# A decoder step on one Trainium2 core: the sample group's attention as plain fp32 products in four column tiles

## The chip, the cores and the metric

The kernel runs on one core of a Trainium2 chip. A core has TensorE (PE in the profile, with its weight loads shown apart as PEld), VectorE (DVE), ScalarE (ACT), GpSimd (POOL), and queues that issue DMAs, most of them from SyncE (SP). The metric is device time in microseconds for one execution, as the median of several runs; lower is better.

## The reference, cut to what matters

The program is one layer of a decoder for a prompt group (1024 rows) and a sample group (8 rows, one new token each, with 4096 past tokens in a paged cache). All is fp32. The change touches the attention of the sample group, which is this part of the reference:

```python
def mla_sample(q_nope, q_rope, c_new, kr_new, pool_ckv, pool_krope, page_table, w_uk, w_uv):
    q_lat = jnp.einsum('bthd,lhd->bthl', q_nope, w_uk)
    past_c = pool_ckv[page_table].reshape(Bd, -1, KV_LORA)      # 8 x 4096 x 256
    past_r = pool_krope[page_table].reshape(Bd, -1, ROPE_DIM)   # 8 x 4096 x 32
    s_past = jnp.einsum('bthl,bkl->bhtk', q_lat, past_c) + jnp.einsum('bthr,bkr->bhtk', q_rope, past_r)
    s_new = jnp.einsum('bthl,bkl->bhtk', q_lat, c_new) + jnp.einsum('bthr,bkr->bhtk', q_rope, kr_new)
    ...
    s = jnp.concatenate([s_past.astype(jnp.float32) * MLA_SCALE, s_new], axis=-1)
    p = jax.nn.softmax(s, axis=-1).astype(c_new.dtype)
    o_lat = jnp.einsum('bhtk,bkl->bthl', p[..., :P], past_c) + jnp.einsum('bhtk,bkl->bthl', p[..., P:], c_new)
    return jnp.einsum('bthl,lhd->bthd', o_lat, w_uv).reshape(Bd, T, H * MLA_HEAD_DIM)
```

There are 8 heads. Keys and values of the prompt's memory, `mem_prompt @ w_xk` and `mem_prompt @ w_xv` (256 rows, 4 heads of 256 columns each), are computed in the same stage, and the layer norm of the convolution's output for its last tiles.

## The kernel before

The program runs its stages one after another: projections and convolution, the prompt group's attention, the sample group's attention (block `c2`, from L617), then the output projection, cross attention and feed-forward. A scheduler sets the order of the instructions on each engine from their dependencies and from the order in which the code gives them; buffers are tiles of pools with a fixed number of copies (`bufs`), and a tile waits until the last user of its copy is done. Most products are in a fast fp32 form, fp32r, of operands split in a rounded high part and the rest as low part (`split`, L136; the cast is `cast`, L127, the subtraction `lows`, L133).

Stage `c2`, for each batch row b of 8 and each of 8 groups g of 4 token tiles (128 tokens each):

- `gather_part` (L634) gathers a quarter of b's latents, 128 partitions x 2048 elements, with an indirect DMA that GpSimd issues; each parity of b has four buffers. `gather_rope` (L629) does the same for the rope keys.
- `score_group` (L711) transposes latents on PE, two banks of four 128x128 tiles (`trc`, L723), splits them into `ch` (ACT) and `cl` (DVE), and multiplies each into `main` with 128 stationary columns: the absorbed queries `qst`, hi and lo, sit in a window of zeros, so that the groups add up on disjoint rows of one PSUM bank (L728, L729). Rope keys go the same way after every fourth group (`trr`, `rh`, `rl`, into `rsc`, L740 and L741).
- `softmax` (L745) copies `main` and `rsc` out (`mr`), turns them with eight plain fp32 products against `summ` (`st`, L753 and L755), takes maximum, exponential and sum, and splits the weights in `pp`.
- `value_group` (L784) splits four token tiles of the latents, not transposed, into `cc` (casts on POOL, low parts on DVE and POOL) and multiplies them with `pp` as 16 stationary columns and 512 moving ones, hi and lo side by side (`pv`, L795). After every second group it gathers a part for b + 2. At the end `ob` is turned with `summ` (L805).

Values of b run beside scores of b + 1. `memory_kv` (L828) has eight heads (keys and values of four) of 48 fp32r products of 256 columns (L140 to L142), with weights cast on ACT and split on DVE; `conv_norm` (L421) norms the last four tiles of the convolution.

Of the kernel before, what the change touches and what calls it, by code (L numbers as in the profile page):

```python
# [9 lines left out]
F32 = mybir.dt.float32  # L10
# [49 lines left out]
def host_constants():  # L60
# [16 lines left out]
    summ = np.zeros((P, 64), np.float32)  # L77
    for a in range(P):
        summ[a, (a // 16) * 8 + a % 8] = 1.0
# [17 lines left out]
def decoder_step(ctx: ExitStack, tc: tile.TileContext, I: dict, O: dict):  # L97
# [11 lines left out]
    class Banks:  # L109
        """PSUM banks of a phase by tag; those that were taken longest ago go to the first tags"""  # L110
# [47 lines left out]

    # constants
# [12 lines left out]
    # residents of the mixer  # L172
# [19 lines left out]
    # memory keys and values; input projections; convolution  # L192
    with ExitStack() as c1:
# [4 lines left out]
        # the attention's half of mix holds small operands until its results come  # L198
# [3 lines left out]
        def to_T(src, rows, dh, dl, c0, he="a", le="v"):  # L202
            """src [rows, 1024] natural -> hi/lo columns c0.. of dh, dl [P, KD, *]"""
# [19 lines left out]
        def load_w(cols, apart=False):  # L223
            """columns of w_in as hi and lo; apart: each range of columns is split on its own"""
# [31 lines left out]
        def small_loads():  # L256
# [4 lines left out]
            # rows of the paged cache, as the gathers take them  # L261
# [13 lines left out]
            # convolution weights, transposed; the state's part of the sample group's convolution  # L275
# [126 lines left out]
        # depthwise convolution  # L402
# [18 lines left out]
    def conv_norm(i, pool_, ps, tag, bufs):  # L421
        """normalisation of the convolution's output over its channels, in place"""
# [7 lines left out]
        V.tensor_scalar(n[:rows], n[:rows], mv[:rows, 0:1], r[:rows], op0=ALU.subtract, op1=ALU.mult)  # L430
        t2 = ps.tile([P, NCT, P], F32, tag="tr", name="tl2")
# [12 lines left out]
    # attention of the prompt group  # L444
    with ExitStack() as c3:
# [145 lines left out]
        for n in range(len(seq) + LAG):  # L591
# [16 lines left out]
            if n in CLN:  # L608
                with tc.high_priority(offset=0):
                    conv_norm(CLN.index(n), ap_, ps, "sc", 1)  # L610
# [4 lines left out]
    # attention of the sample group over the paged cache  # L615
    with ExitStack() as c2:
        ps = Banks(tr=3, st=1, main=1, rsc=1, pv=1, mk=1)  # L617
# [15 lines left out]
        def gather_part(b, c):  # L633
            raw = (dp if b % 2 else ra).tile([P, 8, LAT], F32, tag="raw", bufs=4, name="craw")  # L634
# [8 lines left out]
        # absorbed queries  # L643
# [7 lines left out]
        main, rsc, probs, pvt = {}, {}, {}, {}  # L651

        def score_banks(b):
            main[b] = ps.tile([P, 512], F32, tag="main", name="main")
            rsc[b] = ps.tile([P, 4, P], F32, tag="rsc", name="rsc")

        score_banks(0)
# [8 lines left out]
        ukT = dp.tile([HD, H, LAT], F32, tag="cc", bufs=4, name="ukT")  # L666
# [15 lines left out]
        summ = dp.tile([P, 64], F32, name="summ")  # L682
        nc.sync.dma_start(summ, I["k_summ"])
        # scores of the new token, on every partition
# [14 lines left out]
        # hi | lo columns of the absorbed queries inside windows of zeros  # L699
        ZW, ZR = 112, 64  # L700
        qst = [de.tile([P, 2, 2 * ZW + 16], F32R, name=f"qst{j}") for j in range(2)]
        qrs = [de.tile([P, 2 * ZR + 64], F32R, name=f"qrs{j}") for j in range(2)]
        for j in range(2):
            G.memset(ff(qst[j]), 0.0)
            G.memset(ff(qrs[j]), 0.0)
        olT = kp.tile([P, 2, H, DB], F32, tag="qs", name="olT")

        def score_group(b, g):
            qw, qv = qst[b % 2], qrs[b % 2]
            if g == 0:  # L710
                gather_rope(b)  # L711
                V.tensor_copy(qw[:, :, ZW:ZW + 8], ql[:, :, b, :])
                V.tensor_tensor(qw[:, :, ZW + 8:ZW + 16], ql[:, :, b, :], ff(qw[:, :, ZW:ZW + 8]), op=ALU.subtract)
                for j in range(4):
                    r0, z0 = slice(j * RD, (j + 1) * RD), ZR + 16 * j
                    V.tensor_copy(qv[r0, z0:z0 + 8], qr[:, b, :])
                    V.tensor_tensor(qv[r0, z0 + 8:z0 + 16], qr[:, b, :], ff(qv[0:RD, ZR:ZR + 8]), op=ALU.subtract)
                if b:
                    score_banks(b)
            for k in range(2):  # L720
                t = ps.tile([P, 4, P], F32, tag="tr", name="trc")
                for j in range(4):
                    T.transpose(t[:, j, :], raws[b][g // 2][:, (g % 2) * 4 + j, k * P:(k + 1) * P], ident)  # L723
                ch = de.tile([P, 512], F32R, tag="ch", bufs=3, name="ch")
                cl = de.tile([P, 512], F32R, tag="cl", bufs=3, name="cl")
                split(ch, cl, t.rearrange("p a b -> p (a b)"), "a", "v")
                w = qw[:, k, ZW - 16 * g:ZW - 16 * g + P]
                T.matmul(main[b], w, ch, start=(g == 0 and k == 0), stop=False)  # L728
# [652 lines left out]
```

## Time and profile before

| what | value |
|---|---|
| median of 3 runs | 1978.37 us (1973.42 to 1978.55) |
| span of the profiled execution | 1981.0 us |
| PE busy in it | 1849.9 us, 93% |
| mean granted TensorE clock | 0.960 |
| stage `c2`, first PE instruction to the first of the next stage | 482.33 to 831.47 us |

The page of the profile gives the profiled execution's span, from the first to the last instruction, and no other time of it; the runs' times are of other executions. "Busy" is the time in which at least one instruction of an engine runs. Matmuls overlap their neighbours in the pipeline, so the mean duration of one is longer than the distance from its start to the start of the next. A plain fp32 product has two records. "Releaser" is the instruction whose end let a waiting one go.

### The profile page before, as it was taken

The numbers are of one execution on the slowest core, as the hardware profiler recorded it, in microseconds if no ns is written. First come the engines' busy times: TensorE is split into PE (matmuls) and PEld (weight loads), VectorE is DVE, ScalarE is ACT, GpSimd is POOL, SyncE is SP. The second block draws the span as 40 slices with busy tenths as digits, with TensorE's granted clock in tenths as the row PEclk, the third lists the DMA queues.
The fourth block names the chain that finished last, engine by engine and source line by source line (L and its number), as shares of the span: only waits on it lengthen the run. The fifth ranks groups of instructions, "written<-read, shape, count | busy, mean of one in ns | idle before, by whom it ended". The sixth has DMA issues, their size and how long they took to land.

```text
span 1981.0 us, 29364 instructions
## 1 busy us (share of the span) xinstructions
PE 1849.9 (93%) x11556; PEld 1687.1 (85%) x11556; DVE 1318.0 (67%) x2278; ACT 602.3 (30%) x1317; POOL 640.0 (32%) x636
## 2 busy tenths in 40 slices
PE   8857779998999989799999999999999999999997
PEld 8857777787877777587997787999999999999997
DVE  4999768888788777766547865755455555545447
ACT  3433457776533443411114400211111111111114
POOL 0779973225155545531104522200000101010002
PEclk9978989999998998799999999999999999999999
DMA  6002000005344531322433720211111111111102
GB/s 202 25 23 59 22 12 1 1 12 214 118 145 158 193 133 54 127 76 102 145 98 111 241 81 24 77 52 43 44 43 43 43 54 54 54 44 54 44 1 87
DMA packets 103205, 154.00 MB, mean 78 GB/s; under 512 B 8718, under 2 KB 79798, under 8 KB 98963
## 3 DMA queue, kind: packets, MB, share of 16 engines
q1 hardware_dynamic: 97307, 114.38, 18.4%
q0 software_dynamic: 5760, 37.75, 5.3%
q8 instruction: 91, 1.49, 0.3%
q14 instruction: 47, 0.39, 0.1%
HBM read 140.29 MB, written 12.29 MB: 77 GB/s over the span
## 4 chain that ended last, share of the span: by engine, by line
PE 72%; POOL 12%; DVE 7%; issue 5%; DMA 2%; ACT 2%; SPq 0%; DVEq 0%; POOLq 0%; ACTq 0%
POOL mix L411 7%; PE pd L141 6%; PE pd L142 6%; PE pd L140 6%; PE pu L140 6%; PE pu L141 6%; PE pu L142 6%; PE po L141 3%; PE po L142 3%; PE po L140 3%; PE trc L723 2%; DVE cc L134 2%; PE px L141 2%; PE px L140 2%; PE px L142 2%
## 5 line engine op out<-in xcount | busy, mean ns | idle before, releaser
L1294 DVE TENSOR_TENSOR YT<-YT,pd 128x344 f32<-128x344 f32 (+2 forms) x344 | 171.8, 504 | 232.1 <-PE pd L142 232.1
L141 PE MATMUL pd<-hl,dh 128*128 128x344 f32 (+2 forms) x800 | 251.4, 314 | 2.8 <-DVE hl L134 2.8
L142 PE MATMUL pd<-hh,dl 128*128 128x344 f32 (+2 forms) x800 | 251.4, 314 | 0.0
L140 PE MATMUL pd<-hh,dh 128*128 128x344 f32 (+2 forms) x800 | 250.3, 314 | 0.0
L140 PE MATMUL pu<-XHb,uh 128*128 128x344 f32 x768 | 246.4, 321 | 0.0
L141 PE MATMUL pu<-XLb,uh 128*128 128x344 f32 x768 | 246.0, 320 | 0.0
L142 PE MATMUL pu<-XHb,ul 128*128 128x344 f32 x768 | 245.9, 320 | 0.0
L1281 ACT ACTIVATE r<-pu 128x344 f32<-128x344 f32 x96 | 43.9, 459 | 425.3 <-PE pu L142 383.5
L131 POOL TENSOR_SCALAR dh<-draw 128x1024 fp32r<-128x1024 f32 x32 | 39.2, 1243 | 386.2 <-PE pd L141 385.3
L411 POOL TENSOR_TENSOR mix<-mix,tap 128x512 f32<-128x512 f32 (+1 forms) x120 | 160.4, 1337 | 8.2 <-ACT tap L410 0.8
L416 DVE SCALAR_TENSOR_TENSOR mix<-u,convw,mix 128x768 f32<-128x768 f32 (+1 forms) x120 | 153.9, 1328 | 0.3
L141 PEld LDWEIGHTS pd<-hl,dh 128*128 128x128 f32 x800 | 150.7, 188 | 3.1 <-DVE hl L134 3.1
L142 PEld LDWEIGHTS pd<-hh,dl 128*128 128x128 f32 x800 | 150.8, 189 | 0.0
L140 PEld LDWEIGHTS pd<-hh,dh 128*128 128x128 f32 x800 | 150.2, 188 | 0.0
L142 PEld LDWEIGHTS pu<-XHb,ul 128*128 128x128 f32 x768 | 145.1, 189 | 0.0
L140 PEld LDWEIGHTS pu<-XHb,uh 128*128 128x128 f32 x768 | 145.0, 189 | 0.0
L141 PEld LDWEIGHTS pu<-XLb,uh 128*128 128x128 f32 x768 | 144.8, 189 | 0.0
L131 POOL TENSOR_SCALAR cc<-craw 128x1024 fp32r<-128x1024 f32 x60 | 73.4, 1236 | 130.9 <-PE pv L795 123.3
L410 ACT ACTIVATE tap<-u,convw 128x512 f32<-128x512 f32 (+1 forms) x120 | 73.8, 618 | 103.5 <-POOL mix L411 102.1
L131 POOL TENSOR_SCALAR uh<-uraw 128x1024 fp32r<-128x1024 f32 x32 | 34.2, 1068 | 213.3 <-PE pu L141 119.8
L128 ACT CAST ch<-trc 128x512 fp32r<-128x512 f32 x128 | 72.6, 588 | 95.0 <-PE trc L723 89.7
L134 DVE TENSOR_TENSOR cl<-trc,ch 128x512 fp32r<-128x512 f32 x128 | 84.9, 684 | 23.6 <-ACT ch L128 23.2
(506 smaller groups left out, 4906.3 us busy)
## 6 DMA issues: line engine op xcount, KB each, us to landing
uraw<-in_w_up SPq DMA_DIRECT2D x32, 512.0 KB
draw<-in_w_down SPq DMA_DIRECT2D x32, 512.0 KB
kt<-in_cache_mem_k SPq DMA_DIRECT2D x32, 256.0 KB
vsr<-in_cache_mem_v SPq DMA_DIRECT2D x32, 256.0 KB
xin<-in_x_prompt SPq DMA_DIRECT2D x8, 512.0 KB
wraw<-in_w_in SPq DMA_DIRECT2D x16, 256.0 KB
kraw<-in_w_xk SPq DMA_DIRECT2D x16, 256.0 KB
kraw<-in_w_xv SPq DMA_DIRECT2D x16, 256.0 KB
```

The source lines that it names most:

```text
L128: return A.copy(dst, src)
L131: return G.tensor_scalar(dst, src, 1.0, 1.0, op0=ALU.mult, op1=ALU.mult)
L134: return (V if eng == "v" else G).tensor_tensor(dst, src, ff(hi), op=ALU.subtract)
L140: T.matmul(out, lh, rh, start=start, stop=False)
L141: T.matmul(out, lh, rl, start=False, stop=False)
L142: T.matmul(out, ll, rh, start=False, stop=stop)
L410: A.activation(w[:, :cut], u[:, j:j + cut], AF.Copy, scale=convw[:, ct, j:j + 1])
L411: G.tensor_tensor(acc, acc, w[:, :cut], op=ALU.add)
L416: V.scalar_tensor_tensor(acc, u[:, j + cut:j + S], convw[:, ct, j:j + 1], acc, op0=ALU.mult, op1=ALU.add)
L723: T.transpose(t[:, j, :], raws[b][g // 2][:, (g % 2) * 4 + j, k * P:(k + 1) * P], ident)
L1281: A.activation(r, t, AF.Relu)
L1294: return V.tensor_tensor(y, y, t, op=ALU.add)
```

## The change

In stage `c2` nothing is split any more in the attention: scores and values are plain fp32 products, and each covers only a 32-column tile of the array, four of them side by side. A half e of a batch is 16 token tiles. For a half, `columns` makes all transposes and copies them out (`ct`, `krt`), ACT and DVE in turn; `scores` has 8 products with 32 stationary and 512 moving columns and 16 with 32 and 128, where the product for c = 0 to 3 goes to rows 32c to 32c + 31 of `main`; rope scores are added to the same bank, so `rsc` goes and the turn in `softmax` has four products. `values` has 16 products with the weights `E_` (8 columns) as stationary operand and 256 columns of the gathered latents as moving one, straight from the buffer of the gather. The four partial sums are copied by ACT and DVE and added up in the turn, which has two products. Even batches have five buffers for the gathers. Memory weights are cast on POOL.

PE's order in the stage is written by hand: `softmax`, `values`, `memory_kv` and `conv_norm` are generators that stop where PE should do something else, and a loop of 19 iterations strings them together.

On PE, in the fourth batch, before: score, value, transposing and memory products take turns in small pieces (`ch`, `cl`, `cc`, `rh`, `rl` are split operands):

```order
L740 MATMUL rsc<-rh,qrs_5404 128x128
L741 MATMUL rsc<-rl,qrs_5404 128x128
L795 MATMUL pv<-cc,pp 16x512 x4
L740 MATMUL rsc<-rh,qrs_5404 128x128
L741 MATMUL rsc<-rl,qrs_5404 128x128
L795 MATMUL pv<-cc,pp 16x512 x4
L728 MATMUL main<-ch,qst_5402 128x512
L729 MATMUL main<-cl,qst_5402 128x512
L728 MATMUL main<-ch,qst_5402 128x512
L795 MATMUL pv<-cc,pp 16x512 x4
L723 MATMUL trc<-ident,craw 128x128 x2
L729 MATMUL main<-cl,qst_5402 128x512
```

PE at the end of one iteration and the beginning of the next, after (the second `trc` row reads the next batch's first gathered part):

```order
L146 MATMUL mk<-kwh,ML__5414 128x256
L730 MATMUL trc<-ident,craw 128x128 x16
L734 MATMUL trr<-ident,kr 128x128 x4
L746 MATMUL main<-ct,qst_5401 32x512 x8
L750 MATMUL main<-krt,qrs_5403 32x128 x16
L799 MATMUL pv<-craw,E__5910 8x256 x16
L760 MATMUL st<-summ,mr 128x8x8 x4
L730 MATMUL trc<-ident,craw 128x128 x16
L766 MATMUL st<-ident,mx 8x128
L811 MATMUL pv<-summ,ob_5404 128x8 x2
L144 MATMUL mk<-kwh,MH__5413 128x256
```

The pieces have become blocks: all transposes of half a half, all scores of a half, all values of a half, and the memory products stand in one block between the two blocks of transposes.

POOL in the middle of the stage, before: gathers stand among casts and low parts of the latents:

```order
L131 TENSOR_SCALAR cc<-craw 128x4x256
L631 DMA kr<-in_cache_krope,idx 128x1024
L635 DMA craw<-in_cache_ckv,idx 128x2048
L131 TENSOR_SCALAR cc<-craw 128x4x256
L134 TENSOR_TENSOR cc<-craw,cc 128x4x256
L635 DMA craw<-in_cache_ckv,idx 128x2048
L131 TENSOR_SCALAR cc<-craw 128x4x256 x3
L635 DMA craw<-in_cache_ckv,idx 128x2048
```

and after, where they stand in pairs among the casts of the memory's weights:

```order
L135 TENSOR_SCALAR kwh<-kraw 128x512
L641 DMA craw<-in_cache_ckv,idx 128x2048 x2
L135 TENSOR_SCALAR kwh<-kraw 128x512 x2
L641 DMA craw<-in_cache_ckv,idx 128x2048 x2
L135 TENSOR_SCALAR kwh<-kraw 128x512
L637 DMA kr<-in_cache_krope,idx 128x1024
```

Before, a gather waits for the splits that read its buffer; now it waits for PE's value products, and the casts behind it wait with it.

The diff, cut to its core:

```diff
-    summ = np.zeros((P, 64), np.float32)
-    for a in range(P):
-        summ[a, (a // 16) * 8 + a % 8] = 1.0
+    summ = np.zeros((P, 72), np.float32)
+    for c in range(4):
+        for h in range(8):
+            for e in range(2):
+                summ[32 * c + 8 * e + h, (4 * e + c) * 8 + h] = 1.0
+            summ[32 * c + h, 64 + h] = 1.0
...
-        ps = Banks(tr=3, st=1, main=1, rsc=1, pv=1, mk=1)
+        ps = Banks(tr=3, main=2, st=1, pv=1, mk=1)
...
-            raw = (dp if b % 2 else ra).tile([P, 8, LAT], F32, tag="raw", bufs=4, name="craw")
+            raw = (dp if b % 2 else ra).tile([P, 8, LAT], F32, tag="raw", bufs=4 + (b % 2 == 0), name="craw")
...
+        def columns(b, e):
+            if e == 0:
+                gather_rope(b)
...
+            ct = de.tile([P, 2, 4, 512], F32, tag="ct", bufs=2, name="ct")
+            for c in range(4):
+                if c == 2:
+                    yield
+                g = 4 * e + c
+                for k in range(2):
+                    t = ps.tile([P, 4, P], F32, tag="tr", name="trc")
+                    for j in range(4):
+                        T.transpose(t[:, j, :], raws[b][g // 2][:, (g % 2) * 4 + j, k * P:(k + 1) * P], ident)
+                    cast("av"[k], ct[:, k, c, :], t.rearrange("p a b -> p (a b)"))
...
+        def scores(b, e):
...
             for k in range(2):
+                for c in range(4):
+                    T.matmul(main[b][32 * c:32 * c + 32], qw[:, k, window(e)], ct[:, k, c, :],
+                             start=(e == 0 and k == 0), stop=False)
+            for j in range(4):
+                for c in range(4):
+                    tail["sc"] = T.matmul(main[b][32 * c:32 * c + 32, j * P:(j + 1) * P], qv[:, j, window(e)],
+                                          krt[:, c, :], start=False, stop=(e == 1 and j == 3))
...
+        def values(b, e):
+            E_, sa = probs[b]
...
+            for tt in range(16 * e, 16 * e + 16):
+                r = slice(32 * (tt % 4), 32 * (tt % 4) + H)
+                T.matmul(pvt[b][r, 0:LAT], E_[:, tt, :], raws[b][tt // 8][:, tt % 8, :], start=(tt < 4), stop=(tt >= NTOK - 4))
+            if b + 2 < DB:
+                gather_part(b + 2, 2 * e)
+                gather_part(b + 2, 2 * e + 1)
+            if e == 1:
+                ob = obs[b % 2]
+                for c in range(4):
+                    r = slice(32 * c, 32 * c + H)
+                    cast("av"[c % 2], ob[r], pvt[b][r, 0:LAT])
+                yield
...
+                    T.matmul(ot[:, k, :], ob[:, k * P:(k + 1) * P], summ[:, 64:72], start=True, stop=True)
...
-                split(wh, wl, raw, "a", "v")
+                split(wh, wl, raw, "p", "v")
+                if q == 2:
+                    yield
...
+        with tc.manual_schedule(engines={mybir.EngineType.PE}):
+            for n in range(len(halves) + 3):
+                cols = columns(*halves[n]) if n < len(halves) else iter(())
+                next(cols, None)
+                run(soft)
+                run(ends)
+                next(mem, None)
+                next(cols, None)
+                run(soft)
+                if 1 <= n <= len(halves):
+                    scores(*halves[n - 1])
+                run(soft)
+                if n >= 3:
+                    v = values(*halves[n - 3])
+                    if next(v, ends) is not ends:
+                        ends.append(v)
+                if 1 <= n <= len(halves) and halves[n - 1][1]:
+                    soft.append(softmax(halves[n - 1][0]))
+                    run(soft)
+                if n >= 11 and norms:
+                    next(norms[0], None)
+                    if n % 2 == 0:
+                        next(norms.pop(0), None)
+            run(ends)
```

## Rows read from the trace of the kernel before

**Rows 1.** The page: span, busy time by engine, and the chain that ended last.

```profile
span 1981.0 us, 29364 instructions
...
PE 1849.9 (93%) x11556; PEld 1687.1 (85%) x11556; DVE 1318.0 (67%) x2278; ACT 602.3 (30%) x1317; POOL 640.0 (32%) x636
...
PE 72%; POOL 12%; DVE 7%; issue 5%; DMA 2%; ACT 2%; SPq 0%; DVEq 0%; POOLq 0%; ACTq 0%
```

**Rows 2.** PE's timeline (start, length) at the stage's two ends; L671 by line.

```profile
482.33 1.47 PE L671 MATMUL tuk<-ident,ukn 128*64 128x128 f32 x12
...
L671 PE MATMUL tuk<-ident,ukn 128*64 128x128 f32 x16 | 2.1, 274 | 1.5 <-DVE ukT L672 1.5
...
831.47 1.64 PE L140 MATMUL po<-w_oh,XHb 128*128 128x512 f32 x6
```

**Rows 3.** Windows: busy us (instructions) of PE, PEld, DVE, ACT, POOL; clock, DMA share, GB/s.

```profile
486.00:832.00 346.00, 314.82 (x1920) 252.09 (x1920) 269.59 (x441) 141.12 (x255) 168.53 (x118) 0.90 0.39 132
...
600.00:660.00 60.00, 57.14 (x345) 47.97 (x346) 47.75 (x87) 23.37 (x43) 28.07 (x20) 0.89 0.50 169
660.00:720.00 60.00, 57.03 (x377) 45.12 (x377) 44.72 (x76) 25.18 (x47) 32.73 (x23) 1.00 0.41 141
```

**Rows 4.** PE's timeline: score products, memory products, rope scores and score turns in a row.

```profile
500.12 0.39 PE L728 MATMUL main<-ch,qst 128*128 128x512 f32 x1
500.36 0.39 PE L729 MATMUL main<-cl,qst 128*128 128x512 f32 x1
...
519.99 0.28 PE L140 MATMUL mk<-kwh,MH__5411 128*128 128x256 f32 x1
520.11 0.28 PE L141 MATMUL mk<-kwl,MH__5411 128*128 128x256 f32 x1
...
520.98 0.28 PE L741 MATMUL rsc<-rl,qrs 128*128 128x128 f32 x1
521.10 0.27 PE L740 MATMUL rsc<-rh,qrs 128*128 128x128 f32 x1
...
522.00 1.00 PE L753 MATMUL st<-summ,mr 128*128 128x64 f32 x8
```

**Rows 5.** PE by line, 486 to 832 us: count, busy us, mean ns, idle before and releaser.

```profile
L723 PE MATMUL trc<-ident,craw 128*128 128x128 f32 x512 | 84.0, 290 | 1.8 <-DVE cl L134 1.8
L795 PE MATMUL pv<-cc,pp 128*16 128x512 f32 x256 | 72.2, 412 | 4.9 <-DVE cc L134 4.9
...
L728 PE MATMUL main<-ch,qst 128*128 128x512 f32 x128 | 56.7, 443 | 0.0
...
L140 PE MATMUL mk<-kwh,MH__5411 128*128 128x256 f32 x128 | 38.9, 304 | 4.2 <-ACT kwh L128 4.2
...
L740 PE MATMUL rsc<-rh,qrs 128*128 128x128 f32 x64 | 17.3, 290 | 0.0
...
L753 PE MATMUL st<-summ,mr 128*128 128x64 f32 x64 | 10.5, 321 | 0.0
L805 PE MATMUL pv<-summ,ob 16*128 16x8 f32 x64 | 10.4, 281 | 0.3 <-ACT ob L801 0.3
```

**Rows 6.** Waits, 486 to 832 us: in total, times, longest.

```profile
POOL cc L131 <- PE pv L795: 123.3, 9, 22.5
...
PE main L729 <- DVE cl L134: 11.2, 7, 2.9
...
PE pv L795 <- DVE cc L134: 4.9, 4, 2.4
PE rsc L741 <- DVE rl L134: 4.8, 1, 4.8
```

**Rows 7.** Splits and copies by line, 486 to 832 us (`ukT` 481 to 500).

```profile
L134 DVE TENSOR_TENSOR cl<-trc,ch 128x512 fp32r<-128x512 f32 x128 | 84.9, 684 | 23.6 <-ACT ch L128 23.2
...
L134 DVE TENSOR_TENSOR cc<-craw,cc 128x1024 fp32r<-128x1024 f32 x48 | 82.8, 1753 | 18.3 <-POOL cc L131 18.2
L128 ACT CAST ch<-trc 128x512 fp32r<-128x512 f32 x128 | 72.6, 588 | 95.0 <-PE trc L723 89.7 <-PE main L728 3.8
...
L131 POOL TENSOR_SCALAR cc<-craw 128x1024 fp32r<-128x1024 f32 x57 | 70.4, 1246 | 129.9 <-PE pv L795 123.3 <-PE tql L677 6.3
...
L672 DVE COPY ukT<-tuk 64x512 f32<-64x512 f32 x4 | 2.5, 670 | 0.0
```

**Rows 8.** Gathers: the DMA view (median us from issue to landing), POOL's timeline.

```profile
craw<-in_cache_ckv,idx POOLq DMA_INDIRECT x32, 6.9
...
547.92 1.02 POOL L635 DMA_INDIRECT craw<-in_cache_ckv,idx  x1 [1.34 <-DVE cc L134]
...
554.27 1.82 POOL L635 DMA_INDIRECT craw<-in_cache_ckv,idx  x1 [0.16 <-POOL cc L131]
```

**Rows 9.** The tile `st`: duration ns min/median/max, first and last start.

```profile
L753 PE MATMUL st<-summ,mr x64: 217/275/421, 522.0 to 795.9; 128*128 128x64 f32 x64
...
L755 PE MATMUL st<-summ,mr x64: 217/275/476, 524.8 to 805.9; 128*128 128x64 f32 x64
...
L779 PE MATMUL st<-sm,ones x16: 170/240/361, 539.4 to 813.3; 128*128 128x8 f32 x16
```

More of the change, by code (lines that the diff above doesn't have):

```diff
@@ L609, in decoder_step @@
                 with tc.high_priority(offset=0):
-                    conv_norm(CLN.index(n), ap_, ps, "sc", 1)
+                    for _ in conv_norm(CLN.index(n), ap_, ps, "sc", 1):
+                        pass
         with tc.issue_after(mla_end[-1].ins):
@@ L714, in score_group @@
                 for j in range(4):
[L715 to L719, printed above, removed]
-            for k in range(2):
[L721 to L728, printed above, removed]
-                T.matmul(main[b], w, cl, start=False, stop=(g == 7 and k == 1))
@@ L730, in score_group @@
-            if g % 4 == 3:
-                t = ps.tile([P, 4, P], F32, tag="tr", name="trr")
-                for q in range(4):
-                    T.transpose(t[:, q, :], kraws[b][:, (g - 3 + q) * P:(g - 2 + q) * P], ident)
-                rh = de.tile([P, 4, P], F32R, tag="rh", bufs=1, name="rh")
-                rl = de.tile([P, 4, P], F32R, tag="rl", bufs=1, name="rl")
-                split(rh, rl, t, "a", "v")
-                for q in range(4):
-                    w = qv[:, ZR - 64 * (q % 2):ZR - 64 * (q % 2) + P]
-                    dst = rsc[b][:, (g - 3 + q) // 2, :]
-                    T.matmul(dst, w, rh[:, q, :], start=(q % 2 == 0), stop=False)
-                    tail["sc"] = T.matmul(dst, w, rl[:, q, :], start=False, stop=(q % 2 == 1))
@@ L781, in softmax @@
             V.tensor_tensor(sa, sab, E_[:, NTOK], op=ALU.add)
[L782 to L802 removed]
+            tail["pv"] = V.reciprocal(sa, sa)
@@ L845, in decoder_step, with run, memory_all @@
         mkv = [(h, *n) for h in range(MH) for n in (("w_xk", "new_mem_k"), ("w_xv", "new_mem_v"))]
-        LAG = 2
-        vals = []
-        for b in range(DB):
-            if b == 6:
-                memory_in()
-                for x in mkv:
-                    memory_kv(*x)
-            for g in range(8):
-                score_group(b, g)
-                if g >= LAG and vals:
-                    value_group(*vals.pop(0))
-            while vals:
-                value_group(*vals.pop(0))
-            softmax(b)
-            vals = [(b, g) for g in range(8)]
-        with tc.issue_after(tail["sc"].ins):
-            for i in range(len(CLN), NTL + 1):
-                conv_norm(i, dp, ps, "mk", 2)
-        while vals:
-            value_group(*vals.pop(0))
+        def run(steps):
+            for x in list(steps):
+                if next(x, steps) is steps:
+                    steps.remove(x)
+        def memory_all():
+            for x in mkv:
+                yield from memory_kv(*x)
+                yield
+        memory_in()
+        halves = [(b, e) for b in range(DB) for e in range(2)]
+        norms = [conv_norm(i, dp, ps, "mk", 2) for i in range(len(CLN), NTL + 1)]
+        mem, soft, ends = memory_all(), [], []
+        with tc.manual_schedule(engines={mybir.EngineType.PE}):
[22 more added lines that the diff above has]
+            run(ends)
+            for x in norms:
+                for _ in x:
+                    pass
         pmp.__exit__(None, None, None)
```

85 lines of the change are left out of this document (35 added, 50 removed).

## The prediction

> **What bounds the kernel now.** I read first the page's busy shares and its chain: TensorE is busy for 93% of the span and carries 72% of the chain that ended last [rows 1]. The change touches one stage, so I then took the stage by itself. It begins with the first transpose of the up-projection at 482.33 us and ends with the first product of the output projection at 831.47 us [rows 2], so it lasts 349.1 us. In a window almost as long PE is busy for 314.8 of 346 us, DVE for 269.6, POOL for 168.5 and ACT for 141.1, and the mean granted clock is 0.90 [rows 3]. Thus PE is the bound of the stage. The clock has two levels, 1.2 and 2.4 GHz, so a mean of 0.90 says that cycles worth 0.10 x 346 = 34.6 us of full speed were not granted.
>
> Mean durations of matmuls overlap one another, so I priced PE by the distance from one start to the next at full clock. An fp32r product of 512 columns takes 500.12 to 500.36, some 0.233 us over a burst; an fp32r product of 256 columns takes 519.99 to 520.11, 0.12 us [rows 4]. Twelve fp32 transposes of 128 columns last 1.47 us, and one by itself 0.274, so from one to the next it is (1.47 - 0.274) / 11 = 0.109 us [rows 2]. Eight records of the plain fp32 product that turns scores (64 columns, 128 weight columns) last 1.00 us [rows 4], and the shortest by itself 0.217 [rows 9], so it is (1.00 - 0.217) / 7 = 0.112 us; an fp32r product of 128 columns with as many weight columns takes the same, 520.98 to 521.10 [rows 4]. Counts are from the rows by line [rows 5]. Before: transposes 512 + 64 at 0.109, 62.8 us; score products 256 at 0.233, 59.6; value products 256 at 0.233, 59.6; rope scores 128 at 0.112, 14.3; score turns 128 at 0.112, 14.3; output turns 64 at 0.112, 7.2; memory products 384 at 0.12, 46.1; and some 150 small passes, 15. That makes 279. The other 70 us of the stage are the 34.6 of clock and some 35 of waits and seams.
>
> **What the change takes from PE.** The split products of scores, values and rope go: 59.6 + 59.6 + 14.3 = 133.5 us. Half of the score turns and of the output turns go with them: 7.2 + 3.6 = 10.8. Transposes and memory products keep their number. Together -144.3 us.
>
> **What it adds to PE.** 128 products of 512 columns, 256 of 128 and 256 of 256, all plain fp32. The trace records each plain fp32 product twice: 32 score turns make 64 records on each of two lines [rows 5]. So there are 256 + 512 + 512 passes. The widest plain fp32 product in the trace has 64 columns; no row prices 512. Below stands the fp32r rate, 0.233 for 512 columns, which would give 256 x 0.233 + 512 x 0.06 + 512 x 0.12 = 152 us. Nearer stands the transpose, since it also moves fp32 columns: 0.109 for 128, hence 0.435 for 512 and 0.218 for 256, which gives 111 + 56 + 112 = 279 us one after another. Seams of 0.02 to 0.03 on each pass would make it 313. I take 279.
>
> How many of the four column tiles run together decides everything, and no row of before has a product off the first tile. Bounds: one at a time, 279 us; four at a time, 70. I take two. The two records of one product use the same tile and stand next to each other, so if products start in their order, the second record of tile 0 waits for the first, then tile 1 can start beside it, then its own second record must wait again. Each slot then holds the second pass of one tile and the first of the next: 279 / 2 = 139.5 us.
> The Trainium skill ("TensorE: Matmul & The Clock Gate", Part 3, on what overlaps) says that matmuls start and end strictly in program order, which is what this pairing rests on; no run here shows it yet. It also gives (Part 3, measured speedup) 2.38 times for three column tiles of one pass each; by that figure the 279 us would be an estimated 117 and the sum 22 us shorter.
>
> The array changes between its full and its tiled form some five times in a half of a batch, 80 times in all. If nothing overlaps there, a change costs what a transpose lasts beyond its spacing, 0.290 - 0.109 = 0.18 us [rows 2, 5], some 14 us in all; if it costs nothing, 0. I take 6.
> The Trainium skill ("TensorEngine Tiling (Array Packing)", Key Properties) says that changing the tiling mode drains the engine; by it the 14 would stand and the sum be 8 us longer.
>
> PE's work thus changes by 139.5 + 6 - 144.3 = +1 us.
>
> **Waits that go.** PE waited 11.2 us for the low part of the columns (DVE), 4.9 for the split values and 4.8 for the split rope columns [rows 6]: -21 us. The stage's 128 low parts (684 ns) and 48 value splits (1753 ns) on DVE and the 57 value casts on POOL (1246 ns) go too [rows 7]; POOL was waiting for PE for 123.3 us there [rows 6], and DVE had a fifth of the stage free, so beyond these 21 us their going buys nothing. What comes is small: a copy of 512 columns from PSUM took 588 ns on ACT and 670 on DVE [rows 7], and with four or five of these per half, plus the memory's low parts and the softmax, ACT has some 4 and DVE some 7 us of work in an iteration of 346 / 16 = 21.6. The casts of memory weights move from ACT to POOL, where half the columns of a 1246 ns cast make about 0.62 us; they are queued behind gathers that wait for PE's value products, with nearly an iteration of slack. If that were gone, an iteration would wait for two issues of 1.0 to 1.8 us and a cast.
>
> **Waits that come.** A latent part is now read by the value products themselves, so its buffer comes free only when these have run. For batches 3, 5 and 7 there are four buffers: the first part's is freed by the first eight value products at the end of an iteration, and the transposes that open the next iteration read what is gathered into it. A gather takes 6.9 us from issue to landing [rows 8]. Of that, the last eight value products cover 16 x 0.218 / 2 = 1.7 us and the score turn some 0.5. So PE stands some 4.7 us, in each of the three batches twice: 6 x 4.7 = 28 us (22 to 33). Even batches have a fifth buffer and lose 0 to 1.5 us each. Before, the splits freed the buffers ahead of the products and this wait did not exist. Behind the waiting transposes all of PE's hand-made order is queued, memory products among it.
>
> At the end, the softmax of the last batch has nothing beside it: from the last score turn at 805.9 to the last sum at 813.3 us [rows 9], 7.4 us in which PE then did norms. I take +6 (0 to 10). The start differs by 0 to 6; I take 0.
>
> Clock: the stretch from 660 to 720 us has 57.03 us busy at 1.00, that from 600 to 660 has 57.14 busy at 0.89 [rows 3]. The busy share does not tell the clock, so I keep the 34.6 us as they are, with -17 to +15 for the range.
>
> **The sum.** +1 - 21 + 28 + 6 = +14 us. The profiled span is 1981.0 us [rows 1], 2.6 above the median of 1978.4; on the span this gives 1995, on the median **1992**. Own range: seams 0 to +17, form changes -6 to +8, gathers -6 to +5, ends -6 to +10, clock -17 to +15, which hardly all fall to one side: 1968 to 2025.
>
> **Rivals.**
> Four (or three) tiles together: the tiled passes take 70 to 93 us in place of 139.5, -70 to -47. For it: no row excludes it, and no other engine stands in the way at an iteration of some 18 us. Against it: it needs products to start out of their order, or two records to be taken as one. It gives 1922 to 1945; I take 1925 for it.
> The Trainium skill ("TensorEngine Tiling (Array Packing)", Key Properties) states the rule behind this rival, that different tiles load and multiply in parallel; no row here bears on it.
>
> Tiles hardly overlap, so the change does not do what it says: place, the 1280 passes of scores and values; price, 279 to 313 us in place of 133.5 + 10.8. Fully serial, +140 on my sum, less some 10 because longer value products cover more of the gathers: 2120. At an overlap of 1.3 times, 215 us, it is 2067. For it: every record in this trace runs the array by itself. It decides against the kernel below 279 / (144.3 - 13 - 6 + 6) = 2.13 times: there the time is over 0.3% longer. Above 2.34 times it is over 0.3% shorter. So even my own case lies near the line, on its slow side.
>
> **How the numbers follow.** Pairs 0.45; four or three together 0.30; hardly any overlap 0.25. About 0.3%, 6 us, is what a measurement of this kernel can tell from no change. Of the pairs' 0.45, a clock that recovers or cheap gathers make 0.10 faster, 0.10 lie within 6 us, 0.25 are slower. So faster 0.40, same 0.10, slower 0.50. The range leaves out the best end of the second case (some 0.07) and the serial end of the third (some 0.13): 1915 to 2085.
>
> **What would show it.** In the profile after, the starts of score products: a group of 32x512 passes at 0.22 us from start to start means pairs, 0.11 four together, 0.435 none. PE idle ahead of the transposes released by the gather, some 4 to 5 us six times, shows the buffers; if there is none, the gathers landed early. The rows of DVE and POOL in the stage must fall by half without PE waiting for them. The prediction is wrong if the granted clock of the tiled stretches is mostly the lower level, or if PE's order stands behind casts on POOL.

## The result, and the profile after

The changed kernel takes 1930.78 us (median of 4 runs, 1928.84 to 1931.28) where the kernel before takes 1978.46 us beside it. The ratio is 0.9759, with a 95% interval of 0.9745 to 0.9774: 2.4% faster, 47.7 us. The prediction was 1992 us and "slower" as the likeliest sign. The time lies inside its range of 1915 to 2085, but the direction was forecast wrong; what happened is the rival of four tiles together, for which 1922 to 1945 us stood there.

The page of the changed kernel, to be read against [rows 1] (span, busy time by engine, chain):

```profile
span 1927.1 us, 30016 instructions
...
PE 1776.9 (92%) x12100; PEld 1624.9 (84%) x12100; DVE 1170.6 (61%) x2126; ACT 535.1 (28%) x1201; POOL 531.8 (28%) x594
...
PE 71%; POOL 11%; issue 6%; DVE 5%; DMA 5%; ACT 2%; SPq 0%; POOLq 0%; DVEq 0%; ACTq 0%
```

PE is the bound as before. DVE lost 147 us of work and POOL 108, and DMA went from 2 to 5% of the chain. Of the stage, PE's timeline gives both ends (start, length), as in [rows 2]:

```profile
483.15 1.48 PE L670 MATMUL tuk<-ident,ukn 128*64 128x128 f32 x12
...
780.90 2.91 PE L144 MATMUL po<-w_oh,XHb 128*128 128x512 f32 x6
```

The stage lasts 297.8 us and lasted 349.1: 51.4 us went there, while what follows it took 1142.5 us after and 1145.8 before, to the last busy instruction. So the cause is inside the stage. (The spans of the two profiled executions, 1981.0 and 1927.1 us, differ by 53.9 us, 6 more than the medians do; the profiled execution of the changed kernel is its fastest run, 1.9 us under the median.) PE by line there (busy us, mean ns, idle before and its releaser), against [rows 5]:

```profile
L730 PE MATMUL trc<-ident,craw 128*128 128x128 f32 x512 | 76.5, 310 | 28.4 <-DMA craw<-in_cache_ckv,idx 27.9 <-ACT ct L132 0.5
...
L746 PE MATMUL main<-ct,qst 128*32 128x512 f32 x256 | 30.8, 599 | 0.0
...
L750 PE MATMUL main<-krt,qrs 128*32 128x128 f32 x512 | 16.9, 273 | 0.0
```

Two things are to be seen. The 256 records of scores, with a mean length of 599 ns, were busy for 30.8 us, 0.12 us for each: they ran beside one another. And the transposes, which waited for nothing much before, now wait 27.9 us for gathers. One half of a batch, in PE's timeline:

```profile
560.00 1.96 PE L730 MATMUL trc<-ident,craw 128*128 128x128 f32 x16 [0.16 <-DMA craw<-in_cache_ckv,idx]
561.85 0.66 PE L734 MATMUL trr<-ident,kr 128*128 128x128 f32 x4
562.44 1.92 PE L746 MATMUL main<-ct,qst 128*32 128x512 f32 x16
564.18 1.06 PE L750 MATMUL main<-krt,qrs 128*32 128x128 f32 x32
...
759.99 1.91 PE L799 MATMUL pv<-craw,E__7890 128*8 128x256 f32 x32
761.83 1.11 PE L760 MATMUL st<-summ,mr 128*128 128x64 f32 x8
```

From its start to the start of what follows, a half's score block takes 1.74 us, its rope block 0.87 and its value block 1.84: 4.45 us, 71 us for 16 halves at full clock. The starts of the records inside these blocks, from the same trace, show the pattern (us):

```
scores   562.437 562.443 562.450 562.456   562.890 562.896 562.903 562.910   563.319 ...
rope     564.177 564.185 564.191 564.197   564.287 564.294 564.301 564.307   564.396 ...
values   565.051 565.058 565.065 565.071   565.267 565.274 565.280 565.286   565.482 ...
```

Four start within 20 ns, and the next four when these are through: after 0.43, 0.109 and 0.216 us, just the price of one pass.

The waits of PE by line and releaser (us in total, times, longest), against [rows 6]:

```profile
PE trc L730 <- DMA craw<-in_cache_ckv,idx: 27.9, 8, 5.2
PE st L784 <- DVE sm L781: 5.4, 7, 1.9
PE tl L438 <- DVE cln L434: 5.0, 1, 5.0
PE mk L144 <- POOL kwh L135: 4.4, 2, 4.0
```

### The profile page after: what moved, and what is told of

Read it like the earlier page. It is cut to its first block, busy times and chain, and to the rows that moved or that the text cites. A ratio compares the mean times of both kernels' runs of the same rounds, so it can differ in the third digit from the quotient of the medians.

```text
span 1927.1 us, 30016 instructions
## 1 busy us (share of the span) xinstructions
PE 1776.9 (92%) x12100; PEld 1624.9 (84%) x12100; DVE 1170.6 (61%) x2126; ACT 535.1 (28%) x1201; POOL 531.8 (28%) x594
## 4 chain that ended last, share of the span: by engine, by line
PE 71%; POOL 11%; issue 6%; DVE 5%; DMA 5%; ACT 2%; SPq 0%; POOLq 0%; DVEq 0%; ACTq 0%
POOL mix L415 7%; PE pd L145 6%; PE pd L146 6%; PE pd L144 6%; PE pu L144 6%; PE pu L145 6%; PE pu L146 6%; PE po L144 3%; PE po L145 3%; PE po L146 3%; PE trc L730 2%; DMA craw<-in_cache_ckv,idx 2%; PE px L145 2%; PE px L144 2%; PE px L146 2%
## 5 line engine op out<-in xcount | busy, mean ns | idle before, releaser
L730 PE MATMUL trc<-ident,craw 128*128 128x128 f32 x512 | 76.5, 310 | 28.4 <-DMA craw<-in_cache_ckv,idx 27.9
L730 PEld LDWEIGHTS trc<-ident,craw 128*128 128x128 f32 x512 | 67.0, 160 | 34.0 <-issue 30.1
L1311 ACT ACTIVATE hh<-r 128x344 fp32r<-128x344 f32 x96 | 47.0, 492 | 162.3 <-PE pd L146 159.8
```

What stands on the lines that cost most here:

```text
L1311: A.activation(hh[:, cols], r, AF.Square)
```

## The experiments

**Do products start in their order?** The theory that had failed was that products start strictly one after another in the program's order (O); the rival is that each column tile takes its own products as it comes free (Q). The first run puts all products of a tile in a row before those of the next.

```diff
-            for k in range(2):
-                for c in range(4):
+            for c in range(4):
+                for k in range(2):
...
-            for j in range(4):
-                for c in range(4):
+            for c in range(4):
+                for j in range(4):
...
-            for tt in range(16 * e, 16 * e + 16):
+            for tt in (16 * e + 4 * j + c for c in range(4) for j in range(4)):
```

> The same products, but all of one column tile's products stand in a row before those of the next (scores: 2 products for each tile, rope 4, values 4). Theory Q (each tile takes its products from the order as it comes free, so a product may start ahead of an earlier one of another tile): the time stays within about 10 us of 1931, and starts in the score blocks stay in groups of four, 0.435 us apart. Theory O (products start strictly in their order, and in the changed kernel four run together only because the order goes around the tiles): a score block takes about 16 x 0.435 less three overlaps, 5.7 us in place of 1.74, a rope block 3.2 in place of 0.87, eight value products of two rounds together 6.3 in place of 1.85 for a half; together 10.7 us more for each of 16 halves, minus a few us of gather waits that these hide: about 2080 us.

Measured: 1985.9 us (one run), 55 us over the changed kernel. Neither theory expected that. PE's timeline of one half:

```profile
584.67 1.94 PE L746 MATMUL main<-ct,qst 128*32 128x512 f32 x16
586.41 2.44 PE L750 MATMUL main<-krt,qrs 128*32 128x128 f32 x32
588.78 0.39 PE L784 MATMUL st<-sm,ones 128*128 128x8 f32 x2
589.10 4.51 PE L799 MATMUL pv<-craw,E__6233 128*8 128x256 f32 x32
```

The score block, four records to a tile, is as fast as before: 1.74 us. Rope and value blocks, eight records to a tile, are not: they last 2.44 and 4.51 us where they lasted 1.06 and 1.91. The starts (us) follow. A record in the trace does not name its column tile; tiles are assigned here by the program's order.

```
scores   584.669 584.682 584.695 584.709   585.122 585.135 585.149 585.162   ...
rope     586.410 586.519 586.628 586.737   (one at a time)
         586.846+586.852  586.955+586.985  587.065+587.095  587.174+587.204   (two at a time)
         587.313+587.319  587.422+587.452  587.531+587.561  587.640+587.670
         ...
         588.246 588.355 588.465 588.574   (one at a time)
```

The second tile's first score product starts 13 ns after the first tile's first and 1.3 us ahead of the first tile's last, which stands before it in the program. By this assignment O is wrong. In the rope block the second tile's first record starts only when the first tile's fifth does. That fits one reading: records are handed out in order, a busy tile holds its running record and three more, and a fifth for the same tile holds up all that stands behind it. In the changed kernel only two records for a tile stand next to each other (the two of one product), so nothing is held up; the steps between starts inside a group, 6 to 7 ns there and 13 to 14 ns here with four records to a tile, fit a hand-out of some 3.3 ns for each record. The depth was seen with rope and value products alone; no run tried another size.

**Pairs.** The case that the prediction was worked out for can be made: two column tiles in place of four, the first and the third partial product sharing a tile's rows.

```diff
-                    T.matmul(main[b][32 * c:32 * c + 32], qw[:, k, window(e)], ct[:, k, c, :],
-                             start=(e == 0 and k == 0), stop=False)
+                    T.matmul(main[b][32 * (c % 2):32 * (c % 2) + 32], qw[:, k, window(e, c)], ct[:, k, c, :],
+                             start=(e == 0 and k == 0 and c < 2), stop=False)
...
-                r = slice(32 * (tt % 4), 32 * (tt % 4) + H)
+                r = slice(32 * (tt % 2), 32 * (tt % 2) + H)
```

> The four partial products of scores, rope scores and values go to two column tiles in place of four (the first and the third share a tile's rows); the result is the same. Theory Q and theory O both expect two products together: the tiled passes take 2 x 71.5 = 143 us in place of 71.5, so about 1931 + 71 = 2002 us, less up to 10 because the longer value products cover more of the gathers. This is the case that the prediction was worked out for, so if its other terms were right the time is near 1992. The rival, that the gain came from the other engines' relief and not from the products, expects under 1950.

Measured: 1982.0 us (one run; the kernel before ran beside it in 1974.98 to 1982.41). PE's timeline of one half, and its waits for gathers in the stage:

```profile
632.95 3.63 PE L747 MATMUL main<-ct,qst 128*32 128x512 f32 x16
636.40 1.92 PE L751 MATMUL main<-krt,qrs 128*32 128x128 f32 x32
638.25 0.39 PE L785 MATMUL st<-sm,ones 128*128 128x8 f32 x2
638.57 3.63 PE L800 MATMUL pv<-craw,E__6552 128*8 128x256 f32 x32
642.13 0.33 PE L731 MATMUL trc<-ident,craw 128*128 128x128 f32 x1
```

```profile
PE trc L731 <- DMA craw<-in_cache_ckv,idx: 21.7, 6, 4.3
```

A half takes 3.45 + 1.85 + 3.56 = 8.86 us of tiled passes, 142 in all; 139.5 stood in the prediction. The time came out 10 us under its 1992 and 3.3 us over the 1978.7 of the kernel before beside it: with pairs the change would have been worth nothing that can be measured. So the prediction's other terms together were off by some 12 us (of which the gathers, put at 28 us, make 6), and the overlap brought the rest: from two tiles to four it is 51 us. The relief of the other engines and the end of the waits for split operands are all here as in the changed kernel. By themselves they did not bring the gain.

**No tiles.** Scores with 128 stationary columns, values into the same eight rows; rope stays in tiles.

```diff
-                    T.matmul(main[b][32 * c:32 * c + 32], qw[:, k, window(e)], ct[:, k, c, :],
-                             start=(e == 0 and k == 0), stop=False)
+                    w = 104 - 8 * e - 32 * c
+                    T.matmul(main[b], qw[:, k, w:w + P], ct[:, k, c, :],
+                             start=(e == 0 and k == 0 and c == 0), stop=False)
...
-                r = slice(32 * (tt % 4), 32 * (tt % 4) + H)
+                r = slice(0, H)
```

> Scores and values run without column tiles: scores with 128 stationary columns (queries in a window of zeros, as in the kernel before), values into the first 8 rows one after another; only the rope scores stay in four tiles. If a plain fp32 pass costs what the transposes' rate says (0.435 us for 512 columns, 0.218 for 256), scores take 111 us in place of 28 and values 112 in place of 30: about 1931 + 165 = 2096 us, less up to 15 for gathers that are covered. If passes without tiles cost what fp32r passes cost (0.233 and 0.12), it would be 1931 + 60 + 61 - 58 = 1994.

Measured: 2064.5 us (one run). PE's timeline, and two of its waits in the stage:

```profile
659.03 7.13 PE L747 MATMUL main<-ct,qst 128*128 128x512 f32 x16
666.09 1.08 PE L751 MATMUL main<-krt,qrs 128*32 128x128 f32 x32
667.10 0.39 PE L785 MATMUL st<-sm,ones 128*128 128x8 f32 x2
667.42 7.07 PE L800 MATMUL pv<-craw,E__6550 128*8 128x256 f32 x32
674.42 0.76 PE L730 MATMUL trc<-ident,craw 128*128 128x128 f32 x5
```

```profile
PE trc L730 <- DMA craw<-in_cache_ckv,idx: 11.6, 6, 2.7
...
PE st L785 <- DVE sm L782: 1.9, 1, 1.9
```

7.06 us for 16 passes of 512 columns and 7.00 for 32 of 256: 0.44 and 0.219 us for each, as the transposes' rate had said (0.435 and 0.218). The stage's passes rose by 16 x (5.32 + 5.16) = 168 us and the time by 134 only: transposes waited 11.6 us for gathers in place of 27.9, which leaves some 18 us. The sum of the softmax was waited for 1.9 us in place of 5.4, the last norm (5.0 us in the changed kernel) not at all, and the stage's mean granted clock is 0.94 in place of 0.88, with fewer waits in it; how much each of these gave was not separated. Scores and values in plain fp32 without tiles are thus 86 us slower than the split products of the kernel before.

**The gathers.** The nine buffers as one ring over all batches, with the same room: a part then goes into the buffer of the part nine before it.

```diff
-            raw = (dp if b % 2 else ra).tile([P, 8, LAT], F32, tag="raw", bufs=4 + (b % 2 == 0), name="craw")
+            at = (4 * b + c) % 9
+            raw = (dp if at > 4 else ra).tile([P, 8, LAT], F32, tag="raw", bufs=4 + (at < 5), name="craw")
...
-            if b + 2 < DB:
-                gather_part(b + 2, 2 * e)
-                gather_part(b + 2, 2 * e + 1)
+            for p in (4 * b + 2 * e + 9, 4 * b + 2 * e + 10):
+                if p < 4 * DB:
+                    gather_part(*divmod(p, 4))
```

> The nine buffers of gathered latents are used in one ring over all batches (five in one pool, four in the other, in turn) in place of five for even and four for odd batches; a part is then gathered into the buffer of the part nine before it, which is free about one iteration before the transposes need it. Theory: the 27.9 us that transposes waited for gathers fall under 5 us and the time to about 1931 - 25 = 1906 us (1902 to 1912). Rival: the gathers are bound by the DMAs themselves (0.5 of their time is busy in the stage), so the wait comes back at another place and the time stays over 1920.

Measured: 1890.94 us (1889.08 to 1895.63, 4 runs), ratio to the kernel before 0.9553 (0.9536 to 0.957). That is 40 us less than the changed kernel: more than the 28 us of the wait, and 11 us under the range that was expected. Transposes by line in the ring, and two windows from 540 us to the stage's end, first the changed kernel, then the ring (us, busy us of PE, PEld, DVE, ACT, POOL, then clock, DMA share, GB/s):

```profile
L730 PE MATMUL trc<-ident,craw 128*128 128x128 f32 x512 | 66.5, 279 | 1.7 <-ACT ct L132 0.9 <-DMA craw<-in_cache_ckv,idx 0.4
```

```profile
540.00:780.00 240.00, 197.52 (x2128) 151.48 (x2128) 102.09 (x240) 59.33 (x112) 54.45 (x67) 0.92 0.49 171
```

```profile
540.00:744.00 204.00, 186.69 (x2129) 138.75 (x2129) 98.12 (x240) 59.09 (x112) 51.55 (x64) 0.98 0.59 205
```

The wait is gone and the mean granted clock in the windows rose from 0.92 to 0.98. What a wait does to the clock stands in the changed kernel's timeline:

```profile
605.82 3.65 PE L730 MATMUL trc<-ident,craw 128*128 128x128 f32 x16 [4.58 <-DMA craw<-in_cache_ckv,idx]
...
654.53 3.65 PE L730 MATMUL trc<-ident,craw 128*128 128x128 f32 x16 [5.07 <-DMA craw<-in_cache_ckv,idx]
```

After 4.58 and 5.07 us without work, 16 transposes took 3.65 us where they take 1.96 at 560.00 after a wait of 0.16: PE was granted 1.2 GHz, not 2.4, for these (the granted clock is 0.50 from 605.8 to 609.4 us) and for some of the products behind them. The two windows hold the same work, 2128 and 2129 records on PE. PE is idle for 240 - 197.5 = 42.5 us in the first and for 17.3 in the second, 25.2 less, and it is busy for 10.8 us less. So of the 36 us between the windows 25 are the waits themselves and 11 the slower products behind them. (The cycles that were not granted, 0.08 x 240 = 19 us in the one and 0.02 x 204 = 4 in the other, would say 15 us, but a part of them fell while PE stood idle and cost nothing.)

**The order by hand.** The changed kernel with the scheduler's order on TensorE.

```diff
-        with tc.manual_schedule(engines={mybir.EngineType.PE}):
+        with ExitStack():
```

> The changed kernel with the order of TensorE's instructions left to the scheduler in place of written by hand; all else is the same. Theory: the gain came from the products' length, so without the order by hand the time stays within 15 us of 1931. Rival: the order by hand gives a large part of the 48 us (blocks in tiled form, waits kept apart); then it is over 1950 us. In the scheduler's order the tiled products may stand in other sequences, which the groups of four in the trace would show.

Measured: 1916.81 us (1914.28 to 1918.55, 4 runs), 14 us less than with the order by hand. The sign was not expected. Transposes and scores by line, a piece of PE's timeline, and the stage's windows, first the changed kernel, then this run:

```profile
L730 PE MATMUL trc<-ident,craw 128*128 128x128 f32 x512 | 76.4, 286 | 1.5 <-ACT ct L132 1.1 <-DVE ct L134 0.3
```

```profile
L746 PE MATMUL main<-ct,qst 128*32 128x512 f32 x256 | 55.6, 610 | 0.0
```

```profile
599.68 0.59 PE L746 MATMUL main<-ct,qst 128*32 128x512 f32 x1
600.20 1.09 PE L730 MATMUL trc<-ident,craw 128*128 128x128 f32 x8
601.22 1.04 PE L746 MATMUL main<-ct,qst 128*32 128x512 f32 x2
602.20 0.39 PE L144 MATMUL mk<-kwh,MH__5413 128*128 128x256 f32 x1
```

```profile
486.00:780.00 294.00, 242.52 (x2461) 189.62 (x2458) 124.08 (x288) 74.18 (x139) 67.61 (x89) 0.88 0.51 182
```

```profile
486.00:768.00 282.00, 270.11 (x2463) 179.34 (x2463) 121.02 (x287) 73.58 (x138) 69.56 (x89) 0.95 0.52 187
```

The scheduler sets transposes among other work, so none meets a late gather; but it tears the groups of four apart: the two records from 601.22 us, one product by itself, hold PE for 0.98 us, where eight products in groups take 1.74. The scores are busy for 55.6 us, not 30.8. In the stage PE is busy for 28 us more than with the order by hand and idle for 40 us less, so each order has its fault.

**The ring with the scheduler's order.**

> The ring of nine buffers together with the scheduler's order on TensorE. The order by hand cost 14 us in the changed kernel (1931 against 1917) and the ring gained 40 there. Theory: the order by hand lost only because its opening transposes met the late gathers, and keeping the tiled products in unbroken groups is worth what the torn groups cost under the scheduler (score passes 46.8 us against 27.9, rope and value passes some 10 us more). Then the ring gives the scheduler's order nothing, 1912 to 1920 us, and the order by hand with the ring stays ahead at 1891. Rival: the ring frees both, and the scheduler's order goes under 1895.

Measured: 1907.37 us (1906.43 to 1911.65, 4 runs): 16 us behind the ring with the order by hand, 9 us ahead of the scheduler's order without it. Scores by line:

```profile
L746 PE MATMUL main<-ct,qst 128*32 128x512 f32 x256 | 50.9, 602 | 0.0
```

The ring helped here somewhat more than expected, though there was no wait for gathers to remove; its scores are busy for 50.9 us in place of 55.6, and why they are torn less was not followed up. The order by hand pays, once the gathers are early.

**What the relief of VectorE is worth.** The changed kernel with 128 idle subtractions on VectorE.

```diff
                     cast("av"[k], ct[:, k, c, :], t.rearrange("p a b -> p (a b)"))
+                    V.tensor_tensor(scr, ct[:, k, c, :], ct[:, k, c, :], op=ALU.subtract)
```

> The changed kernel with 128 subtractions of 128x512 elements on VectorE added, one behind each copy of transposed columns, on the copy and into a scratch tile that nobody reads: about the 128 x 0.684 = 88 us that the low parts took before. It tells what the relief of VectorE is worth by itself. Theory (the relief buys only the waits that named it): VectorE goes from 8 to 13 us of work in an iteration of 18.6 us, and the time rises by less than 10 us, to at most 1941. Rival (the relief is a main part of the gain): over 1955 us.

Measured: 1941.83 us (1940.53 to 1943.72, 4 runs), 11 us more, just over the bound given. The waits of PE name the place:

```profile
PE trc L732 <- DMA craw<-in_cache_ckv,idx: 27.9, 8, 5.3
PE st L787 <- DVE sm L784: 15.0, 8, 2.1
```

The sum of the softmax comes later behind the added work (15.0 us in place of 5.4). The added work keeps VectorE busy for 89 us, of the 147 that it lost by the change. So the load of the low parts is worth some 11 us of the 48 in this order, not the main part. The run does not bring back PE's 21 us of waits for split operands [rows 6], which went because there are none to wait for, and what the relief of GpSimd and ScalarE is worth was not tested by itself.

**Two further moves on the ring.** The first memory products behind the first half's transposes, and the sum of each softmax behind the value products:

```diff
-                next(mem, None)
+                if n:
+                    next(mem, None)
                 next(cols, None)
+                if not n:
+                    next(mem, None)
...
                     scores(*halves[n - 1])
-                run(soft)
                 if n >= 3:
...
+                run(soft)
```

> The ring of nine buffers (1890.9 us) with two more moves in TensorE's order: the first memory products stand behind all transposes of the first half, and the broadcast of each softmax's sum stands behind the value products. Expected: the 6.5 us that TensorE waited seven times for the sum go down to under 2, the 4.8 us for the first memory weights by 1 to 4; so 1882 to 1887 us. If the waits only move to the next dependency (the exponential ahead of the value products), it stays at 1889 to 1893.

Measured: 1893.52 us (1890.96 to 1895.5, 4 runs): nothing against the ring's 1890.94. The 6.5 us went, and others came. PE's timeline at the start, and its waits:

```profile
510.22 1.09 PE L734 MATMUL trr<-ident,kr 128*128 128x128 f32 x4 [6.21 <-DMA kr<-in_cache_krope,idx]
```

```profile
PE trc L730 <- DMA craw<-in_cache_ckv,idx: 5.9, 4, 2.6
```

The first rope gather, which the work ahead of it had covered, was now waited for itself, and transposes met late latents again, four times; why these came later was not traced. The last run adds one more edit to that:

```diff
-                    cast("av"[c % 2], ob[r], pvt[b][r, 0:LAT])
+                    cast("a" if b == DB - 1 else "av"[c % 2], ob[r], pvt[b][r, 0:LAT])
```

> As the run before, and the four copies of the last batch's value sums all go to ScalarE, since the last of them waited 4.7 us on VectorE behind a split for the next stage, and TensorE 5.4 us for it. Expected: 3 to 5 us less than the run before, 1878 to 1884 us. If the split on VectorE then delays the next stage by as much, no difference.

Measured: 1893.2 us (1889.83 to 1893.8, 4 runs): no difference, as allowed for. The next stage's first product was waiting for its weights anyway:

```profile
743.26 2.07 PE L144 MATMUL po<-w_oh,XHb 128*128 128x512 f32 x4 [6.27 <-POOL w_oh L135]
```

## Why the prediction was wrong, step by step

- **The step that failed: "I take two".** Tiled passes were put at 279 / 2 = 139.5 us, and 71 were measured. The reason given was that the second record of a product must start before the next tile's first can. It does not hold: as the tile-major run is read above, records wait at their own tile, up to three behind the running one, and the next tile's go past them. With 71 in the place of 139.5 the prediction's sum is 1924 us; 1930.8 was measured. The Trainium skill ("TensorE: Matmul & The Clock Gate", Part 3) says that matmuls are monotone in start and end; in the tile-major run a record started 1.3 us ahead of one that stands before it in the program, so by these runs that does not hold for records of different column tiles. The rule of the Trainium skill that stood by the rival ("TensorEngine Tiling (Array Packing)", Key Properties: different tiles work in parallel) agrees with the starts in groups of four.
- **The price of a pass** was right: 0.435 us for 512 columns from the transposes, 0.43 measured; 0.218 for 256, 0.216 measured; serial scores and values, 223 us expected, 225 measured without tiles (16 x 14.06).
- **Changes of form**, 6 us taken: about right. From its start to the next start, the last transpose ahead of a score block holds PE for 0.201 us (median), and in the run without tiles for 0.109, so going into the tiled form costs 0.09 us. The last value passes ahead of a score turn hold it for 0.309 us in place of 0.216, so coming out costs as much. With two to four changes in a half that is 3 to 6 us.
- **Gathers**, 28 us for six waits. The mechanism was right: the waits came ahead of both halves of batches 3, 5 and 7, as forecast, six of 3.7 to 5.2 us (with two of 0.2 and 0.3 they make 27.9), and the ring removed them. That the size agrees is luck. The 28 us were worked out for pairs, and in the run with pairs the six waits came to 21.7 us. With four tiles the last eight value products cover 0.92 us of a gather in place of 1.7, and the same sum gives 6 x 5.5 = 33. So each wait was put about 1 us too long, and the shorter value products made that up. What was left out is the price in clock, 11 us by the two windows above.
- **Waits that go**, 21 us: all three are gone. In their place came 5.4 for the softmax's sum, which was not listed; the 4.4 for memory weights stood there before too (4.2).
- **The relief of DVE**, put at nothing beyond these waits: some 11 us by the run with idle work, mostly the softmax's sum.
- **Clock**, kept at 34.6 us not granted: over 486 to 782 us it was 0.12 x 296 = 36 us. The sum held, its parts did not: the window from 486 to 540 us has a mean of 0.72 after and 0.94 before, so the start lost more and the rest less.
- **Start and end**, +6: not separated. At the end PE waited 5.0 us for the last norm and 1.9 for the last softmax's sum.
- **The slower rival** (hardly any overlap, 2120 us serial) was priced somewhat high: without tiles for scores and values, rope still tiled, the run's expectation from the prediction's rates was 2096 us, or 2081 with gathers that are covered, and 2064.5 was measured.

One error of judgement is worth naming. The case with the largest difference in the outcome rested on an argument about issue order for which no row existed, and it was given the largest chance nonetheless. The point at which the sign turns, put at an overlap of 2.13 to 2.34 times, lies lower: with two tiles (1.97 times) the prediction's sum gives some 17 us on the slow side, and the run came out 3.3 us there, which a measurement of this kernel cannot tell from no change. A straight line between the runs with two and with four tiles meets the kernel before at some 137 us of tiled passes, 2.0 times (an estimate from two runs, one of them single).

## What to carry to other kernels

Thin fp32 products (8 to 32 stationary columns here) that go around four column tiles cost about a quarter of what their passes cost one after another: plain fp32 in four tiles (71 us) beat split fp32r products over the whole array (133.5 us), and without tiles it lost (225 us for scores and values alone). Keep the tiles taking turns: eight records in a row for one tile held up the others, four did not. A scheduler that mixes full-width products in made the scores busy for 51 to 56 us in place of 31. When a product reads a gathered buffer directly, the buffer comes free a step later; count which part is freed last and needed first, and rotate all buffers in one ring (here 40 us, with the same nine buffers).

## What the runs showed of the hardware

A record for a column tile that is busy does not hold up those behind it until four are with that tile (one running, three waiting), if tiles are assigned to records by the program's order: in the tile-major rope block the records from 586.410 to 586.737 us run alone and then in pairs, the value block shows the same, and a score block with four records to a tile lost nothing. Starts inside a group are 6 to 7 ns apart with two records to a tile and 13 to 14 ns with four. A plain fp32 pass of 512 columns takes 0.43 us in two tiles at once, in four at once and over the whole array alike (0.44 there, with the change of form); one of 128 columns takes 0.109 us alone in a tile and with four at once. And a wait of 4 to 5 us on PE was followed by transposes at 0.213 us in place of 0.109, the lower clock level. The ring took away 25 us of idle time and, with it, 11 us of such slower work.
